# Depthwise convolution of a Conformer stage: four of eight chunks without TensorE blocks, and the whole stage in one written order

## The chip, the cores and the metric

The kernel runs on one core of one Trainium2 chip. The metric is the device time of one execution in microseconds (us), the median of several runs. The engines named below are TensorE (PE in the profile, its weight loads PEld), VectorE (DVE), ScalarE (ACT), GpSimd (POOL) and SyncE (SP, which here only issues DMAs). Each engine works through its own queue of instructions in order; semaphores tie the queues together.

## The reference, cut to what matters

A trunk of two layers over 512 positions of 1024 channels, batch 1, all in fp32. The change touches the first part of layer 1, the Conformer module:

```python
def conformer_conv(x, norm, w1, b1, dw_w, dw_b, ln_g, ln_b, w2, b2):
    h = rms_norm(x, norm) @ w1 + b1      # 1024 -> 2048
    h = jax.nn.glu(h, axis=-1)           # value half * sigmoid(gate half)
    h = causal_dwconv(h, dw_w, dw_b)     # width 31, each channel by itself
    h = jax.nn.silu(layer_norm(h, ln_g, ln_b))
    return h @ w2 + b2
```

Each layer then has a cross-attention into 256 memory tokens, whose keys and values (`m @ wk`, `m @ wv`) depend on the memory alone and can be computed ahead, and a gated MLP.

## The kernel before

**Layout.** Channels lie on partitions, positions along the free axis: 1024 channels are 8 chunks of [128, 512]. Matrix products keep fp32 accuracy by splitting both operands into a high part (fp32r, rounded) and a low part (the residual) and adding three matmuls, `mm3` (lines 183 to 185). A weight piece of 128 output channels, [128, 1024], passes through `load_w`: a DMA on SP into `raw` (3 buffers, line 149), a copy on ScalarE for the high part (line 163), a subtraction on VectorE or GpSimd for the low part (line 164), into `whi` and `wlo` (4 buffers each). A piece that is "parked" is split in two halves of 512 into the pool `act` (32 tiles) instead.

**Scheduling.** Outside of `manual_schedule` blocks a scheduler orders each engine's instructions by priority. Inside such a block the listed engines issue exactly in the order in which the code writes the instructions.

**The stage.** `conformer` follows the first layer's MLP. In order:

- Four weight pieces of `pw1` are split (gate and value half of chunks 0 and 1), and four of the eight key pieces for the next cross-attention, parked during the MLP, are multiplied (`mem.keys`). Beside them the RMS norm is formed (`Scaled`): scale (VectorE, line 265), high part (ScalarE, line 173), low part (VectorE, line 178), one chunk after the other.
- `project` multiplies one piece with the eight normed chunks: 24 matmuls of 512 columns. The gate half goes through a sigmoid with its bias on ScalarE (`gate`, line 1349). `gated` multiplies the value half with it on VectorE into a tile `h` with four spare columns in front (line 1362); GpSimd clears those four columns (line 1361).
- The 31 taps of chunk c are shared out. `PE_GROUPS[c]` groups of four taps go to TensorE: `gated` makes four stacked copies of `h` by DMA (`actf<-h`, line 1369, on SP), each with one 32-channel quarter four times, shifted by 0 to 3 positions (they read three of the cleared columns); `spread` builds the matching small diagonal weights on GpSimd (line 1381); `conv_pe` runs 4 matmuls a group into a PSUM bank (line 1391; these are fp32 and show as two records each). The next `N_POOL` taps are products on ScalarE (lines 1410 and 1413) which GpSimd adds into a tile z (line 1414). The rest are taps on VectorE, each a multiply-add onto the PSUM bank (line 1416). `merge` adds bank, bias and z (line 1425). The banks of the convolution come from the pool `aux`, which has two.
- With `PE_GROUPS = [3, 2, 3, 2, 3, 3, 3, 8]` and 5 taps aside for chunks 0 to 6, VectorE has 14 or 18 taps of each of the first seven chunks, 106 in all, and none of the last, whose 31 taps all lie on TensorE. VectorE and GpSimd cannot begin a chunk's PSUM part before its TensorE block.
- The last part is in a manual schedule: keys 6 and 7, the last block, then the LayerNorm over channels. Its sums (`quarters`, line 293; `mu`, then `mean`, line 1497) need all eight merged chunks; between its steps TensorE works through `mem.sums` (line 442), the products of the next cross-attention's value weights `wv`, pieces 0 to 7 (`mem.piece`). After the first sums VectorE subtracts the mean (line 1499) and ScalarE squares (line 1501).

Of the kernel before, what the change touches and what calls it, by code (L numbers as in the profile page):

```python
# [15 lines left out]
P = 128  # L16
# [19 lines left out]
PE_GROUPS = [3, 2, 3, 2, 3, 3, 3, 8]  # L36
N_POOL = [5] * 7 + [0]
LAG = 5

KE = 4  # L40
WINDOWS = (2, 4, 8, 16)
# [5 lines left out]
    ("c_dw_w", (TAPS - 4 * min(PE_GROUPS)) * C), ("c_dw_b", C), ("c_ln_g", C), ("c_ln_b", C), ("c_b_pw2", C),  # L47
# [12 lines left out]
def trunk(ctx: ExitStack, tc: tile.TileContext, I: dict, out: list):  # L60
# [173 lines left out]
    class Scaled:  # L234


        def __init__(self, gain):
            self.gain, self.x, self.ss = gain, [None] * C, None

        def feed(self, c):  # L240
            sq = tmp_f()
            A.activation(sq, X[c], AF.Square)
# [26 lines left out]
        def high(self, c):  # L269
            self.x[c] = self.x[c], high(self.x[c])  # L270
# [18 lines left out]
    def quarters(ps, xs):  # L289

        def quarter(j):
            n = len(xs) - 4 + j
            return PE.matmul(ps[32 * j : 32 * j + 32], onesf[:, :32], xs[n], start=n < 4, stop=n >= 4)


        with tc.issue_after(quarter(3).ins):
            for j in range(3):
                quarter(j)
# [500 lines left out]
    def ffn(layer, norm, nxt, seven):  # L799
# [267 lines left out]
        if nxt:  # L1067
            mem = Memory(1)
            mem.operand(0)
            mem.operand(1)  # L1070
            mem.outputs()
            parked = []
            for n in range(KE):
# [268 lines left out]
    def conformer(norm, nxt, mem, parked):  # L1342
# [4 lines left out]
        def gate(c, psb):  # L1347
            b = tmp_f()
            A.activation(b, psb, AF.Sigmoid, bias=col("c_b_pw1", C + c))
            return b  # L1350

        def pieces(c):
            return load_w(I["pw1"][C + c], V if c == 2 else G), load_w(I["pw1"][c], G)

        def glu(c, w):
            b = gate(c, project(w[0], c, norm.x))
            gated(c, b, project(w[1], c, norm.x))

        def gated(c, b, psa):
            h = tmp.tile([P, T + 4], F32, tag="h", name=nm("h"), bufs=4)  # L1360
            G.memset(h[:, :4], 0.0)
            V.scalar_tensor_tensor(h[:, 4:], psa, col("c_b_pw1", c), b, op0=ALU.add, op1=ALU.mult)
            stacked = [act_f() for _ in range(4)]
            for j in range(4):

                v = h[32 * j : 32 * j + 32, 1 : 1 + T].unsqueeze(1).broadcast_to([32, 4, T])
                dims = [list(d) for d in v.ap]
                dims[1][0] = 1
                nc.sync.dma_start(stacked[j], bass.AP(v.tensor, v.offset, dims))
            hs[c] = h[:, 4:], stacked  # L1370

# [31 lines left out]
        def conv(c):  # L1403
            h, ps = hs[c][0], accs[c]
            z = act_f()
            first = 4 * PE_GROUPS[c]
            for s in range(first, first + N_POOL[c]):
                if s == first:
                    G.memset(z[:, :s], 0.0)
                    A.activation(z[:, s:], h[:, : T - s], AF.Copy, scale=tap(s, c))  # L1410
                else:
                    f = tmp_f()
                    A.activation(f[:, s:], h[:, : T - s], AF.Copy, scale=tap(s, c))
                    G.tensor_tensor(z[:, s:], z[:, s:], f[:, s:], op=ALU.add)
            for i, s in enumerate(range(first + N_POOL[c], TAPS)):
                V.scalar_tensor_tensor(ps[:, s:], h[:, : T - s], tap(s, c), ps[:, s:], op0=ALU.mult, op1=ALU.add)
                if i == LAG and pend:
                    merge(*pend.pop())
            if pend:
                merge(*pend.pop())  # L1420
            pend.append((c, z, ps))

        def merge(c, z, ps):
            if N_POOL[c]:
                V.scalar_tensor_tensor(z, ps, col("c_dw_b", c), z, op0=ALU.add, op1=ALU.add)
            else:
                A.activation(z, ps, AF.Identity, bias=col("c_dw_b", c))
            outs.append(z)
            if c % 4 == 3:
                quarters(mu, outs)  # L1430

        pend, taps = [], [None] * C
        accs = [None] * C
        w = [load_w(I["pw1"][n]) for n in (C, 0, C + 1, 1)]
# [5 lines left out]
        spread(0)  # L1440
        spread(1)
        with tc.high_priority(URGENT):
            for c in range(C):
                norm.split(c)
        ps = project_all(w[:3], norm.x)
        gated(0, gate(0, ps[0]), ps[1])
        gated(1, gate(1, ps[2]), project(w[3], 1, norm.x))
        mu = stat_ps()
        w = pieces(2)
        for c in range(C - 1):  # L1450
            b = None
            if c == 0:
                b = gate(2, project(w[0], 2, norm.x))
            if c == 1:
                gated(2, gate2, project(w[1], 2, norm.x))
                w = pieces(3)
            elif c > 1:
                glu(c + 1, w)
                if c < C - 2:
                    w = pieces(c + 2)  # L1460
            gate2 = b
            if c in (0, C - 2):
                mem.keys(KE + c // 6)
            conv_pe(c)
            if c < C - 2:
                spread(c + 2)
            conv(c)
        xs = [None] * C
        with tc.manual_schedule(engines=ORDERED):
            w = [mem.key_piece(n) for n in (KE + 2, KE + 3)]  # L1470
            mem.eng = G
            ready = [mem.piece(i, park=True) for i in range(3)]
            for n in range(2):
                mem.keys(KE + 2 + n, w[n])
            ready.append(mem.piece(3, park=True))
            last = conv_pe(C - 1)
            ps = [[mm_ps(), mm_ps()] for _ in range(2)]
            z = act_f()
            A.activation(z, accs[C - 1], AF.Identity, bias=col("c_dw_b", C - 1))
            merge(*pend.pop())  # L1480
            outs.append(z)
            mem.eng = None
            ready += [mem.piece(i) for i in (4, 5)]
# [7 lines left out]
            quarters(mu, outs)  # L1491
# [6 lines left out]
            for c in range(C):  # L1498
# [3 lines left out]
                if c == 3:  # L1502
                    go(3)
                    quarters(var, sqs)
# [3 lines left out]
            quarters(var, sqs)  # L1508
# [214 lines left out]
def _layout(inputs):  # L1723
# [3 lines left out]
    a["c_dw_w"] = a["c_dw_w"][:, : TAPS - 4 * min(PE_GROUPS)]  # L1727
# [51 lines left out]
```

## Time and profile before

| | us |
|---|---|
| median of 3 runs | 1447.76 |
| the three runs | 1447.96, 1447.76, 1445.3 |
| the profiled execution | 1445.47 |
| its span, first to last instruction | 1443.0 |
| TensorE busy in the span | 1433.5 |
| first projection of the stage begins | 745.0 |
| last convolution block ends | 870.6 |
| last sum of the mean begins | 873.6 |

The page of the profile is read by sections: section 1 gives the busy time of each engine, a table by stretches the same for parts of the span with the granted TensorE clock (1.00 is full speed), the chain of waits the work that ended last at each moment, and the lists in order of time each engine's instructions: start, length, line, output and inputs, count, and in brackets the idle time before and what ended it. TensorE's instructions are pipelined, so a new one begins before the last ends; the pitch from start to start is what counts. The same holds, more weakly, for VectorE and ScalarE.

### The profile page before, as it was taken

To read this page: it belongs to the slowest core of one execution; us is meant where nothing else is said; L and a number is where in the kernel's file an instruction comes from. 1 tells how busy PE (TensorE), PEld (TensorE's weight loads), DVE (VectorE), ACT (ScalarE), POOL (GpSimd) and SP (SyncE) were. 2 spreads that over 40 slices of the span, in tenths; PEclk is the share of its full clock that TensorE was granted. 3 is DMA by queue.
4 is the path that set the end of the run, shared out by engine and by line. 5 is a ranking of instruction groups with operands and counts; after the bars stand their busy time and mean duration, and the time that the engine had idled before them with its cause. 6 is when DMAs were issued, how large, how long until landed. Compare 5 with 4: busy or idle time off the path is not lost.

```text
span 1443.0 us, 22827 instructions
## 1 busy us (share of the span) xinstructions
PE 1433.5 (99%) x8608; PEld 1260.1 (87%) x8608; DVE 1162.5 (81%) x1916; ACT 787.3 (55%) x1305; POOL 274.8 (19%) x307
## 2 busy tenths in 40 slices
PE   9999999999999999999999999999999999999997
PEld 8888888988899999999887676899888999999997
DVE  6987775768788888888875897878788888888885
ACT  7668754657544444444545447666664444444433
POOL 0012300100022212212006841010001222221201
PEclk9999999999999999999999999999999999999999
DMA  8522232532567777876526654335245777777741
GB/s 303 190 88 89 89 130 73 125 96 88 161 151 166 185 157 166 181 168 146 158 88 177 165 155 151 112 81 138 90 124 128 173 183 159 168 182 163 160 126 59
DMA packets 80398, 205.33 MB, mean 142 GB/s; under 512 B 8992, under 2 KB 10272, under 8 KB 80288
## 3 DMA queue, kind: packets, MB, share of 16 engines
q1 hardware_dynamic: 53504, 155.36, 34.6%
q0 software_dynamic: 26496, 48.25, 20.4%
q8 instruction: 67, 1.10, 0.3%
q14 instruction: 43, 0.35, 0.1%
q10 hardware_dynamic: 288, 0.27, 0.1%
HBM read 145.13 MB, written 2.10 MB: 102 GB/s over the span
## 4 chain that ended last, share of the span: by engine, by line
PE 95%; DVE 2%; ACT 1%; DMA 1%; issue 0%; POOL 0%; SPq 0%; DVEq 0%; POOLq 0%; ACTq 0%
PE mm L183 23%; PE mm L184 23%; PE mm L185 23%; PE aux L183 7%; PE aux L184 7%; PE aux L185 7%; PE mm L442 3%; PE aux L1391 2%; PE aux L515 0%; DMA raw<-in_wv 0%; DVE wlo L164 0%; POOL tmp L1234 0%; DMA raw<-in_wdown 0%; ACT whi L163 0%; PE stat L316 0%
## 5 line engine op out<-in xcount | busy, mean ns | idle before, releaser
L183 PE MATMUL mm<-act,whi 128*128 128x512 f32 (+2 forms) x1093 | 385.3, 354 | 0.3 <-ACT act L849 0.3
L184 PE MATMUL mm<-act,whi 128*128 128x512 f32 (+2 forms) x1093 | 385.0, 352 | 0.1
L185 PE MATMUL mm<-act,wlo 128*128 128x512 f32 (+2 forms) x1093 | 384.7, 352 | 0.0
L183 PEld LDWEIGHTS mm<-act,whi 128*128 128x128 f32 x1093 | 206.3, 189 | 35.1 <-issue 3.3
L184 PEld LDWEIGHTS mm<-act,whi 128*128 128x128 f32 x1093 | 206.6, 189 | 29.4 <-DVE act L164 1.0
L185 PEld LDWEIGHTS mm<-act,wlo 128*128 128x128 f32 x1093 | 206.6, 189 | 27.1
L779 ACT ACTIVATE bigr<-raw 128x512 fp32r<-128x512 f32 x160 | 100.5, 629 | 158.5 <-DMA raw<-wa 67.8
L185 PE MATMUL mm<-bigr,bigr 128*128 128x256 f32 x640 | 181.1, 283 | 0.0
L184 PE MATMUL mm<-bigr,bigr 128*128 128x256 f32 x640 | 181.1, 283 | 0.0
L183 PE MATMUL mm<-bigr,bigr 128*128 128x256 f32 x640 | 180.9, 283 | 0.0
L168 DVE TENSOR_TENSOR tmp<-mm,tmp 128x256 f32<-128x256 f32 x322 | 130.9, 419 | 34.1 <-PE mm L185 27.8
L183 PE MATMUL aux<-act,whi 128*128 128x512 f32 x399 | 156.3, 392 | 0.0
L184 PE MATMUL aux<-act,whi 128*128 128x512 f32 x399 | 156.2, 392 | 0.0
L185 PE MATMUL aux<-act,wlo 128*128 128x512 f32 x399 | 155.2, 389 | 0.0
L163 ACT ACTIVATE whi<-raw 128x1024 fp32r<-128x1024 f32 (+1 forms) x95 | 96.2, 1019 | 96.7 <-PE mm L184 64.7
L786 DVE TENSOR_TENSOR bigr<-raw,bigr 128x512 fp32r<-128x512 f32 x160 | 109.9, 688 | 33.3 <-ACT bigr L779 31.2
L164 DVE TENSOR_TENSOR wlo<-raw,whi 128x1024 fp32r<-128x1024 f32 (+1 forms) x84 | 103.0, 1230 | 31.5 <-ACT whi L163 31.4
L184 PEld LDWEIGHTS mm<-bigr,bigr 128*128 128x128 f32 x640 | 122.7, 192 | 1.6
L183 PEld LDWEIGHTS mm<-bigr,bigr 128*128 128x128 f32 x640 | 122.7, 192 | 1.6
L185 PEld LDWEIGHTS mm<-bigr,bigr 128*128 128x128 f32 x640 | 122.7, 192 | 0.0
L789 POOL DMA_DIRECT2D raw<-raw x46 | 39.8, 866 | 359.3 <-DVE wlo L786 316.0
L793 POOL DMA_DIRECT2D raw<-wa x46 | 39.7, 864 | 302.4 <-DVE bigr L786 252.5
(338 smaller groups left out, 2958.4 us busy)
## 6 DMA issues: line engine op xcount, KB each, us to landing
raw<-wa POOLq DMA_DIRECT2D x138, 256.0 KB, 4.5
big<-in_wdown SPq DMA_DIRECT2D x42, 512.0 KB, 6.7
wa<-in_wpair SPq DMA_DIRECT2D x80, 256.0 KB, 3.4
raw<-in_wpair SPq DMA_DIRECT2D x40, 512.0 KB, 5.7
raw<-in_pw SPq DMA_DIRECT2D x24, 512.0 KB, 3.5
raw<-raw POOLq DMA_DIRECT2D x46, 256.0 KB, 7.5
raw<-in_win SPq DMA_DIRECT2D x20, 512.0 KB, 3.3
raw<-in_wk SPq DMA_DIRECT2D x16, 512.0 KB, 4.2
```

The lines of the kernel that those rows point to most:

```text
L163: A.activation(hi, src, AF.Copy)
L164: fetched[1] = (eng or V).tensor_tensor(lo, src, hi.bitcast(F32), op=ALU.subtract)
L168: V.tensor_tensor(out, a, b, op=ALU.add)
L183: PE.matmul(ps, wh, xh, start=first, stop=False)
L184: PE.matmul(ps, wh, xl, start=False, stop=False)
L185: PE.matmul(ps, wl, xh, start=False, stop=last)
L442: PE.matmul(p, m[j], x, start=k == 0 and j == 0 and x is hi, stop=k == C - 1 and x is lo)
L779: A.activation(self.w[name][0], self.block(name), AF.Copy)
L786: V.tensor_tensor(lo, self.block(name), hi.bitcast(F32), op=ALU.subtract)
L789: G.dma_start(self.r, self.z, accum_op=ALU.add)
L793: G.dma_start(self.r, self.a22, accum_op=ALU.add)
L1391: return PE.matmul(accs[c][32 * j : 32 * j + 32, s:], taps[c][:, 4 * g + j], hs[c][1][j][:, : T - s], start=s == 0, stop=g == PE_GROUPS[c] ...
```

## The change

It rewrites the stage up to the LayerNorm.

- **The sharing of taps.** `PE_GROUPS` becomes `[0, 0, 4, 0, 4, 0, 3, 6]`: chunks 0, 1, 3 and 5 have no block, no diagonal weights and no stacked copies. VectorE begins them itself, by a product of tap 0 written to the bank, and does 26 taps; ScalarE and GpSimd do five taps aside for every chunk, the last too. All 31 taps' weights are loaded in columns.
- **The stacked copies** are issued on ScalarE's queue instead of SP's.
- **The norm** has its instructions on VectorE and ScalarE in a written order: scale of chunk c + 1 between scale and low part of chunk c. Two empty activations load the square root's and the sigmoid's tables ahead.
- **Weights.** The splits of all pieces from the fifth on, the last four key pieces among them, lie on GpSimd; of the value pieces, 0 and 1 are split there whole, 2 and 3 parked there, 4 and 5 parked on VectorE.
- **One order.** Projections, sigmoids, GLU products, taps, taps aside, merges, blocks, keys and weight splits of the whole stage stand in one manual schedule on TensorE, ScalarE, VectorE and GpSimd, written as a script. Its letters: G and V are the gate and value projection of a chunk (G with its sigmoid), S the GLU product with the clearing and the four stacked copies, T a number of VectorE taps, P a number of taps aside, M the merge, F the split of the next weight piece on GpSimd, C the TensorE block, W its diagonal weights, K a key product, Q a half of the mean's sums. The first digit is the chunk, the rest a count.

```diff
-PE_GROUPS = [3, 2, 3, 2, 3, 3, 3, 8]
-N_POOL = [5] * 7 + [0]
-LAG = 5
+PE_GROUPS = [0, 0, 4, 0, 4, 0, 3, 6]
+N_POOL = 5
...
-        def gated(c, b, psa):
+        def gated(c):
             h = tmp.tile([P, T + 4], F32, tag="h", name=nm("h"), bufs=4)
-            G.memset(h[:, :4], 0.0)
-            V.scalar_tensor_tensor(h[:, 4:], psa, col("c_b_pw1", c), b, op0=ALU.add, op1=ALU.mult)
-            stacked = [act_f() for _ in range(4)]
-            for j in range(4):
-
+            if PE_GROUPS[c]:
+                G.memset(h[:, :4], 0.0)
+            V.scalar_tensor_tensor(h[:, 4:], psa[c], col("c_b_pw1", c), b[c], op0=ALU.add, op1=ALU.mult)
+            stacked = []
+            for j in range(4 if PE_GROUPS[c] else 0):
+                stacked.append(act_f())
                 v = h[32 * j : 32 * j + 32, 1 : 1 + T].unsqueeze(1).broadcast_to([32, 4, T])
                 dims = [list(d) for d in v.ap]
                 dims[1][0] = 1
-                nc.sync.dma_start(stacked[j], bass.AP(v.tensor, v.offset, dims))
+                A.dma_start(stacked[j], bass.AP(v.tensor, v.offset, dims))
             hs[c] = h[:, 4:], stacked
+            aside[c] = set_aside(c)
...
+        def shifts(c):
+            ss = list(range(4 * PE_GROUPS[c], TAPS))
+            at = 0 if PE_GROUPS[c] else 1
+            return ss[at : at + N_POOL], ss[:at] + ss[at + N_POOL :]
...
+        def conv(c):
+
+            h, (_, own) = hs[c][0], shifts(c)
+            ps = accs[c] = accs[c] or aux_ps()
+            for s in own:
+                if s:
+                    V.scalar_tensor_tensor(ps[:, s:], h[:, : T - s], tap(s, c), ps[:, s:], op0=ALU.mult, op1=ALU.add)
+                else:
+                    V.tensor_scalar(ps, h, tap(s, c), None, op0=ALU.mult)
+                yield
...
-        with tc.high_priority(URGENT):
+        with tc.high_priority(URGENT), tc.manual_schedule(engines={mybir.EngineType.Activation, mybir.EngineType.DVE}):
+            norm.scaled(0)
             for c in range(C):
-                norm.split(c)
...
+                norm.high(c)
+                if c + 1 < C:
+                    norm.scaled(c + 1)
+                norm.low(c)
+        warm("gates", AF.Sigmoid, norm.copied[3])
...
+            run("S0 G1 F0 P02 F0 P03 T015 V1 F0 S1 T011 P12 F0 G2 P13 F0 T15 M0 V2 S2 W4 F0 P22 G3 F0 P23")
+            run("T114 V3 S3 T17 F0 C2 P32 G4 F0 P33 T25 M1 T25 T34 V4 S4 F0 P42 T31 M2 G5 F0 P43 W6 T313 V5 S5 F0 P52")
+            run("T38 C4 T45 M3 T45 G6 F0 P53 T53 V6 S6 F0 P62 T52 M4 Q0 G7 F0 P63 W7 T516 V7 S7 F0 P72 T55 C6")
+            run("T63 K4 P73 T62 M5 K5")
+            ready = [mem.piece(i) for i in range(2)]
+            run("T64 K6 C7 T65 M6 T72 M7 K7")
+            ready += [mem.piece(i, park=True) for i in (2, 3)]
             ps = [[mm_ps(), mm_ps()] for _ in range(2)]
-            z = act_f()
-            A.activation(z, accs[C - 1], AF.Identity, bias=col("c_dw_b", C - 1))
-            merge(*pend.pop())
-            outs.append(z)
             mem.eng = None
-            ready += [mem.piece(i) for i in (4, 5)]
+            ready += [mem.piece(i, park=True) for i in (4, 5)]
             steps = mem.sums(0, ps[0], ready)
```

More of the change, by code (lines that the diff above doesn't have):

```diff
@@ L1072, in ffn @@
             parked = []
-            for n in range(KE):
+            for n in range(PARKED):
                 if n + 1 < C // 2:
@@ L1449, in conformer @@
[L1449 to L1467, printed above, removed]
+                norm.high(c)
@@ L1468, in conformer @@
+                if c + 1 < C:
+                    norm.scaled(c + 1)
+                norm.low(c)
+        warm("gates", AF.Sigmoid, norm.copied[3])
         xs = [None] * C
+        mem.eng = G
         with tc.manual_schedule(engines=ORDERED):
[L1470 to L1475, printed above, removed]
@@ L1476, in conformer, with run @@
-            last = conv_pe(C - 1)
+            ps0 = project_all([ws["G0"], ws["V0"]], norm.x)
+            mu = stat_ps()
+            def run(script):
+                for step in script.split():
+                    k, c, n = step[0], int(step[1]), int(step[2:] or 0)
+                    if k == "G":
+                        sigmoid(c, project(ws[step], c, norm.x))
+                    elif k == "V":
+                        psa[c] = project(ws[step], c, norm.x)
+                    elif k == "S":
+                        gated(c)
+                    elif k == "T":
+                        convs[c] = convs[c] or conv(c)
+                        for _ in range(n):
+                            next(convs[c])
+                    elif k == "P":
+                        for _ in range(n):
+                            next(aside[c])
+                    elif k == "M":
+                        assert next(convs[c], True) and next(aside[c], True)
+                        merge(c)
+                    elif k == "F":
+                        weights(G)
+                    elif k == "C":
+                        conv_pe(c)
+                    elif k == "W":
+                        spread(c)
+                    elif k == "K":
+                        mem.keys(c, ws.get(step, parked[c] if c < PARKED else None))
+                    elif k == "Q":
+                        quarters(mu, outs, c)
```

90 lines of the change are left out of this document (41 added, 49 removed).

## The prediction

> **What bounds the kernel now.** I read the page first, then the table by stretches over the convolution stage, then the chain of waits through it, then each engine's instructions in time.
>
> ```profile
> span 1443.0 us, 22827 instructions
> PE 1433.5 (99%) x8608; PEld 1260.1 (87%) x8608; DVE 1162.5 (81%) x1916; ACT 787.3 (55%) x1305; POOL 274.8 (19%) x307
> ```
>
> ```profile
> core 0: us, PE busy (x) PEld busy (x) DVE busy (x) ACT busy (x) POOL busy (x), PEclk, DMA share, GB/s
> 800.00:820.00 20.00, 20.00 (x96) 15.11 (x96) 18.59 (x30) 7.90 (x12) 17.02 (x15) 1.00 0.76 208
> ```
>
> TensorE has hardly a gap, so a microsecond of TensorE work taken out is a microsecond won, if nothing else makes TensorE wait. In this stage two engines stand right behind it: VectorE at 18.6 of 20 and GpSimd at 17.0 of 20. ScalarE looks free, but only as long as nothing in its queue has to wait. The median of the runs, 1447.76, lies 2.3 us above the profiled execution's 1445.47, and the lowest run 0.2 below it. My sum is made against 1445.47; the 2.3 goes into the range.
>
> **TensorE's part.** The chain gives the durations.
>
> ```profile
> 785.49 0.43 PE mm L183
> ...
> 796.64 2.69 PE aux L1391 x24
> ...
> 857.84 0.32 PE mm L183
> ...
> 863.78 6.82 PE aux L1391 x64
> 870.60 2.99 PE mm L442 x12
> 873.59 1.00 PE stat L293 x8
> 874.58 1.59 PE mm L442 x6
> 876.17 0.86 PE aux L1497 x2
> 877.03 4.12 PE mm L442 x18
> ```
>
> A convolution block of three groups takes 2.69, of eight 6.82: (6.82 - 2.69) / 5 = 0.83 a group and 0.2 besides. The first matmul after a block takes 0.43 where its neighbours take 0.23: 0.2 more. Between 785.49 and 796.64 lie two projections: (11.15 - 0.2) / 2 = 5.45 each. Two key products lie between 857.84 and 863.78: 2.9 each. Before, groups 3, 2, 3, 2, 3, 3, 3, 8 make 27 x 0.83 + 8 x 0.2 = 24.0. After, 4, 4, 3, 6 make 17 x 0.83 + 4 x 0.2 = 14.9. That is 9.1 less, and four switches fewer save 0.8: **9.9 us off TensorE**, the whole gain.
>
> **VectorE's part.** Taps rise from 106 to 140, and the last chunk's sum comes over from ScalarE.
>
> ```profile
> 784.35 8.48 DVE L1416 SCALAR_TENSOR_TENSOR aux<-h,par,aux 128x488 f32<-128x488 f32 x13
> 792.75 0.74 DVE L1425 SCALAR_TENSOR_TENSOR actf<-aux,par,actf 128x512 f32<-128x512 f32 x1
> 793.41 2.27 DVE L1416 SCALAR_TENSOR_TENSOR aux<-h,par,aux 128x493 f32<-128x493 f32 x3
> ...
> 877.54 4.86 DVE L1499 TENSOR_TENSOR actf<-actf,aux 128x512 f32<-128x512 f32 x8
> ```
>
> ```profile
> L1416 DVE SCALAR_TENSOR_TENSOR aux<-h,par,aux 128x491 f32<-128x491 f32 (+16 forms) x106 | 72.4, 727 | 3.6 <-PE aux L1391 2.3
> ```
>
> A tap lasts 0.727, but each begins before the last has ended: thirteen start 8.4 before the merge, 0.65 a tap, and 0.66 for a merge or a GLU product (792.75 to 793.41). The new taps are four chunks of 26, two of 10, one of 14, one of 2. 140 x 0.65 + 16 x 0.66 + 4 key residuals under 0.5 = 103 us. The new chunks need no block, so VectorE begins when chunk 0's two products are there. The projections start here:
>
> ```profile
> 745.02 0.40 PE L183 MATMUL mm<-act,whi 128*128 128x512 f32 x1
> ```
>
> Two products instead of three: 745.0 + 10.9 = 755.9. 756.3 + 103 = 859.3, beside TensorE's 755.9 + 104.5 = 860.4 for the same stretch (14 projections, blocks, four keys, one sum). Balanced with no room: VectorE hides its 34 taps only if it never stands still. The norm's pitch falls from three instructions in turn (scale, copy, residual) to VectorE's two, some 1.3, and its table loads move ahead. Both gain nothing by themselves: the first four keys hold TensorE until 745.0, and six matmuls a chunk (5.45 / 4 = 1.36) then consume no faster than that. Without the pipelining the copy's 0.6 and its hand-overs would stand in each chunk's pitch, and two products at a time would wait up to 8 x 0.7 = 5.6.
>
> **GpSimd and ScalarE: where the change adds waits.** These rows price them.
>
> ```profile
> 798.79 2.41 POOL L164 TENSOR_TENSOR wlo<-raw,whi 128x1024 fp32r<-128x1024 f32 x1
> 801.12 0.12 POOL L1409 MEMSET actf<- 128x12 f32 x1
> 801.19 5.30 POOL L1414 TENSOR_TENSOR actf<-actf,tmp 128x499 f32<-128x499 f32 x4
> 806.44 2.42 POOL L164 TENSOR_TENSOR wlo<-raw,whi 128x1024 fp32r<-128x1024 f32 x1
> ...
> 863.76 7.51 POOL L164 TENSOR_TENSOR act<-raw,act 128x512 fp32r<-128x512 f32 x6
> ```
>
> ```profile
> 792.55 2.50 ACT L1413 ACTIVATE tmp<-h,par 128x499 f32<-128x499 f32 x4
> 796.45 1.06 ACT L163 ACTIVATE whi<-raw 128x1024 fp32r<-128x1024 f32 x1 [1.40 <-PE mm L184]
> 797.41 0.70 ACT L1410 ACTIVATE actf<-h,par 128x500 f32<-128x500 f32 x1
> ...
> 863.82 0.38 ACT L163 ACTIVATE bigr<-mm 128x256 fp32r<-128x256 f32 x1 [2.49 <-PE mm L185]
> ...
> 872.52 1.06 ACT L163 ACTIVATE whi<-raw 128x1024 fp32r<-128x1024 f32 x1 [0.21 <-DMA raw<-in_wv]
> 874.74 0.60 ACT L1493 ACTIVATE tmp<-stat 128x512 f32<-128x512 f32 x1 [1.15 <-PE stat L293]
> ```
>
> ```profile
> 786.52 4.31 SPq L1369 DMA_DIRECT2D actf<-h  x4
> ```
>
> ```profile
> L1369 SPq DMA_DIRECT2D actf<-h x32: 554/890/1922, 766.4 to 855.8; - x32
> ```
>
> ```profile
> actf<-h SPq DMA_DIRECT2D x32, 256.0 KB, 4.8
> ```
>
> A weight residual on GpSimd takes 2.33 (798.79 to 801.12), an add 1.31 (801.19 to 806.44 for four). A weight copy on ScalarE takes 0.96, a tap copy 0.6. GpSimd's queue now holds 20 pieces (15 before) and 32 adds (28): 18 x 2.33 + 4 x 1.25 + 32 x 1.31 + spreads of 4 = 93 us in a stage of 100.
>
> In that queue stands the clearing of four columns of h, written inside the GLU step. The stacked copies read those columns. They were issued by SP, whose wait held up weight loads only; now ScalarE issues them, and waits in its written order. Behind it there: the next weight copy (GpSimd's next residual waits for it), the tap copies, the next sigmoid (VectorE's next GLU product waits), and in the end the keys' copies.
>
> Chunk 2: G1 ends at 761.4, its sigmoid and the copy of G2 take ScalarE to 763.2, and GpSimd starts then. Written ahead of the clearing are five residuals and eight adds: 5 x 2.33 + 8 x 1.31 + 0.2 = 22.3, so it comes at 785.7. VectorE has h ready at 779.4. Four issues take 4.31: if the first two take the shortest, some 0.6, the others take 1.55, and the last starts 2.7 in, at 788.6, and lands 4.8 later, at 793.4. TensorE reaches the block at 788.6: **4.9 us of stall**. An issue of 0.55 or 1.92 throughout would give 3.8 or 7.9; I take the burst's 4.31, which is this very transfer.
>
> From there GpSimd and ScalarE hold each other up in turn: each burst (4.3) and the next weight copy (1.0) leave GpSimd idle. Next residual 791.2; four residuals and eight adds (19.8) and two or three clears and gaps: clearing for chunk 4 at 811.5. Burst and copy to 816.9; as much again with chunk 6's spread: 838.0. Burst and copy to 843.4; two residuals, four adds, a spread of 2: chunk 7's clearing at 855.5. Its burst ends at 859.8; K7's weights and two tap copies follow, and only at 862.3 is key 4's high part out of ScalarE. VectorE, which has stood before key 4's residual since 853.2, then does it, two taps and chunk 5's merge: 864.7. Chunk 7's block needs the bank that this merge frees. TensorE is there at 793.5 + 63.7 (two blocks of 3.73, eight projections, the sum, a block of 2.9, three keys) = 857.2: **7.5 us of stall**.
>
> The mean: key 7 ends, then follow in written order ScalarE's copy of it (0.5), a piece of wv in two copies, its residuals on GpSimd (0.6 + 2 x 1.25), the load of piece 5 into that buffer, piece 5's two copies, and the copy of the sums. From the buffer's release to the first copy took 3.75 in the run before: of the six residuals from 863.76, at 1.25 each, the fourth ends piece 2 at 868.8, and the copy of piece 5, three buffers on, starts at 872.52. In all 0.5 + 0.6 + 2.5 + 3.75 + 1.1 + 0.6 and some 0.2 of hand-overs = 9.3, against 2.99 + 1.00 + 1.59 = 5.6 on TensorE: **3.7 us**. Piece 6's residual then delays the eight subtractions (0.6 each) behind the 4.12 of products: **1.1**.
>
> Sum: -9.9 + 4.9 + 7.5 + 3.7 + 1.1 = +7.3; 1445.5 + 7.3 = **1452.8**, rounded to 1453. Free are the 16 stacked copies fewer on SP (it only waits less) and the 64 more columns of parameters, loaded at the start and not read before 756.
>
> One rule speaks for a smaller price. The Trainium skill, "DMA: Bandwidth & Descriptors", section "Issuing engines are not separate DMA queues", says that issuing on another engine saves only the sequencer's time to initiate, usually small beside the transfer. The burst's 4.31 beside 4.8 is not small; by the rule the bursts would hold ScalarE little, and the sum would be that of the short issues below, 1446.7.
>
> **The rivals.** *The clearing does not bind* (the copies go out as soon as h is there). Then the first two stalls vanish, the last two stay: -9.9 + 4.8 = -5.1, **1440.4**, faster. For it: VectorE and TensorE are balanced at 859 to 860; against it: the rows' 22.3 us of GpSimd work. It decides once the clearing comes within 5 us after h. If the wv pieces come early too, it is the full -9.9, 1435.6.
>
> *Short issues*: four at about 0.6 on ScalarE's own queue. Bursts shrink by 1.9, chunk 7's clearing comes at 851.2, key 4's copy at 856.2, the merge ends at 858.5, and TensorE is there at 856.2: stalls 4.0 + 2.3 + 3.7 + 1.1 = 11.1 against 9.9, **1446.7**, no change. Against it: SP's burst, the same transfers with nothing else in between.
>
> *VectorE becomes the bound* without the coupling: if the taps did not overlap, at 0.727, it would end 140 x 0.077 = 11 us later. The blocks wait for banks that its merges free, and the sums for its last merge, so all of it but the 2 or 3 us that TensorE's products behind the last block cover comes through, some 8.5; the last two stalls stay: -9.9 + 8.5 + 4.8 = +3.4, **1448.9**. It loses from a pitch of 0.70 on. The 8.48 for thirteen speaks against it.
>
> *TensorE's clock falls in the gaps.* Each window above grants 1.00, but none has a gap; after gaps of 4.9 and 7.5, the blocks behind them (3.7 and 5.4) could run at half speed, 0 to +9.1, middle **1457**. The Trainium skill, "TensorE: Matmul & The Clock Gate", section "HAM oscillation — how this bites in real kernels", says that idle gaps over about 3.4 us halve the clock; no run here shows it.
>
> **How the numbers follow.** Coupling as summed 0.42 (its own range 1449 to 1456); coupling and slow clock 0.13; VectorE 0.05; short issues 0.13; clearing not binding 0.20; full gain 0.07. 0.2% is about 2.9 us, what a measurement of this kernel can tell from no change. Faster: 0.27; same: 0.13; slower: 0.60. The range from 1440 to 1457.5 takes in the first rival and the middle of the last; the full gain, half of the slow clock and issues of 1.92 (+21) stay out.
>
> **What would show it.** Right: in the changed profile TensorE idles before chunk 2's and chunk 7's blocks, released by the stacked copies and by VectorE; ScalarE idles before its issues, released by a GpSimd memset some 6 us after VectorE wrote h; GpSimd idles before residuals, waiting for ScalarE's copies; VectorE idles some 9 us before key 4's residual; the mean stands 3 to 4 us late. Wrong: blocks that start at once, memsets that run early, a burst of four below 2.5 us, or taps at another pitch than 0.65.

## The result, and the profile after

| | us | to the kernel before |
|---|---|---|
| before, median of 6 runs | 1446.39 | |
| after, median of 6 runs | 1458.84 (1458.23 to 1459.39) | 1.0085 [1.0072, 1.0098] |
| after, the profiled execution | 1458.82 | 13.35 above the profiled execution before |

The change makes the kernel slower by 12.45 us. The direction was predicted; the time lies 6 above the predicted 1453 and 1.3 above the end of the range.

The page of the changed kernel: span and busy time of each engine.

```profile
span 1457.0 us, 22652 instructions
PE 1431.0 (98%) x8528; PEld 1259.7 (86%) x8528; DVE 1186.3 (81%) x1948; ACT 789.0 (54%) x1311; POOL 287.3 (20%) x307
```

TensorE has less to do than before (1433.5) and the span is 14 longer: it waits, where before it hardly did. What TensorE waited for between 740 and 900, with the total, the number and the longest wait:

```profile
PE aux L1389 <- DVE actf L1432: 7.0, 1, 7.0
PE aux L1389 <- DMA actf<-h: 4.9, 2, 4.6
PE aux L1525 <- ACT tmp L1521: 3.3, 1, 3.3
PE aux L295 <- ACT tmp L1529: 0.3, 1, 0.3
```

The first three are the three large stalls of the prediction: 4.9 before chunk 2's block was forecast and 4.6 came, 7.5 before chunk 7's and 7.0 came, 3.7 before the mean and 3.3 came. The last is what came of its fourth term, 1.1 behind the mean. The instructions in time show the mechanism (start, length, engine, line, operation; idle time before and its releaser in brackets):

```profile
745.97 0.40 PE L183 MATMUL mm<-act,whi 128*128 128x512 f32 x1
...
786.51 0.10 POOL L1358 MEMSET h<- 128x4 f32 x1
786.64 4.33 ACTq L1366 DMA_DIRECT2D actf<-h  x4
794.30 5.30 PE L1389 MATMUL aux<-actf,big 128*32 128x512 f32 x32 [4.63 <-DMA actf<-h]
...
857.55 0.11 POOL L1358 MEMSET h<- 128x4 f32 x1
857.69 4.33 ACTq L1366 DMA_DIRECT2D actf<-h  x4
864.21 0.36 ACT L163 ACTIVATE bigr<-mm 128x256 fp32r<-128x256 f32 x1
864.61 0.42 DVE L164 TENSOR_TENSOR bigr<-mm,bigr 128x256 fp32r<-128x256 f32 x1 [3.06 <-ACT bigr L163]
866.35 0.75 DVE L1432 SCALAR_TENSOR_TENSOR actf<-aux,par,actf 128x512 f32<-128x512 f32 x1
867.20 8.05 PE L1389 MATMUL aux<-actf,big 128*32 128x512 f32 x48 [7.02 <-DVE actf L1432]
...
886.96 2.08 PE L1525 MATMUL aux<-tmp,fourth 128*128 128x512 f32 x2 [3.32 <-ACT tmp L1521]
```

GpSimd clears the four columns at 786.5 (forecast 785.7), ScalarE issues its four copies at once and is held for 4.33 (forecast 4.31), the block starts at 794.3 (793.4). In the end the same chain frees chunk 7's bank: clearing, burst, key 4's copy, its residual, chunk 5's merge. It runs 2.0 to 2.5 later than forecast. Two of the signs that the prediction named came out much smaller: the clearing for chunk 2 stands 2.9 behind the end of VectorE's product, not some 6, and VectorE stands 3.06 before key 4's residual, not some 9. VectorE is later than the prediction had it: that product ends at 783.6, not at 779.4.

Two rows were not in the sum. The first is the length of the blocks. Four groups should take 3.5, six 5.2; they took 5.30 and 8.05. The table by stretches has the reason in its column PEclk (after the stretch, its length and five engines' busy times comes the granted clock, then DMA share and GB/s):

```profile
core 0: us, PE busy (x) PEld busy (x) DVE busy (x) ACT busy (x) POOL busy (x), PEclk, DMA share, GB/s
786.00:788.00 2.00, 2.00 (x11) 1.65 (x10) 1.93 (x3) 0.00 (x0) 1.62 (x3) 1.00 0.32 33
...
796.00:798.00 2.00, 2.00 (x16) 0.70 (x12) 1.89 (x4) 2.00 (x4) 2.00 (x1) 0.56 0.51 203
...
870.00:872.00 2.00, 2.00 (x12) 0.46 (x8) 1.96 (x4) 0.00 (x0) 2.00 (x2) 0.50 0.00 0
...
888.00:890.00 2.00, 2.00 (x5) 1.29 (x4) 0.43 (x1) 1.06 (x1) 0.00 (x0) 0.52 1.03 416
```

After each of the three gaps the clock stands at 0.5 to 0.6 for some microseconds, and the work behind the gap runs on it.

The second is the pitch of the taps. In the view of one line's instructions, between 784 and 793, the kernel before has these thirteen taps (shortest, median and longest duration in ns, first and last start, shapes):

```profile
L1416 DVE SCALAR_TENSOR_TENSOR aux<-h,par,aux x13: 716/729/735, 784.4 to 792.1; 128x488 f32<-128x488 f32 x1, 128x487 f32<-128x487 f32 x1, 128x499 f32<-128x499 f32 x1, 128x486 f32<-128x486 f32 x1
```

and the changed kernel these:

```profile
L1426 DVE SCALAR_TENSOR_TENSOR aux<-h,par,aux x13: 732/739/744, 783.5 to 792.8; 128x502 f32<-128x502 f32 x1, 128x501 f32<-128x501 f32 x1, 128x500 f32<-128x500 f32 x1, 128x499 f32<-128x499 f32 x1
```

A tap lasts the same, but twelve intervals take 7.7 before (0.65 each with the first, 0.64 without) and 9.3 after (0.775 each). The shapes tell the two apart. A tap at shift s works on 512 - s positions. Before, 488 and 487 are one chunk's; from there on the taps of two chunks take turns (487, 499, 486, ...). After, 502, 501, 500, 499 are one chunk's, each adding onto the bank that the last one writes. In the program such a tap carries a wait for VectorE's own count of the tap before it. The first taps of the row of before, one by one (the last line holds two taps), have both pitches already:

```profile
784.35 0.72 DVE L1416 SCALAR_TENSOR_TENSOR aux<-h,par,aux 128x488 f32<-128x488 f32 x1
785.11 0.73 DVE L1416 SCALAR_TENSOR_TENSOR aux<-h,par,aux 128x487 f32<-128x487 f32 x1
785.75 1.37 DVE L1416 SCALAR_TENSOR_TENSOR aux<-h,par,aux 128x499 f32<-128x499 f32 x2
```

From 488 to 487, in one chunk, it is 0.76; from 487 to 499, to the other chunk, 0.64. At 0.775 the 140 taps would take some 108 us, not 91 (an estimate: a few of them follow an instruction of another chunk). In the chain of waits from 780 to 900 VectorE's taps have the largest share:

```profile
by line: DVE aux L1426 37.3%; issue 14.5%; ACTq L1366 6.9%; PE aux L1389 6.7%; POOL act L164 4.3%; ACT tmp L1529 3.8%; ACT whi L163 3.5%; POOL actf L1417 2.9%; DMA raw<-in_wv 2.6%; DVE h L1359 2.4%; DVE actf L1432 2.3%; ACT tmp L1416 2.0%; 
```

That leaves two suspects for the loss, the late clearing and the dependent taps, and a third, the clock, for the 6 us between sum and result.

### The profile page after: what moved, and what is told of

Its sections match the earlier page's. It is cut to its first block, busy times and chain, and to the rows that moved or that the text cites. A ratio compares the mean times of both kernels' runs of the same rounds, so it can differ in the third digit from the quotient of the medians.

```text
span 1457.0 us, 22652 instructions
## 1 busy us (share of the span) xinstructions
PE 1431.0 (98%) x8528; PEld 1259.7 (86%) x8528; DVE 1186.3 (81%) x1948; ACT 789.0 (54%) x1311; POOL 287.3 (20%) x307
## 4 chain that ended last, share of the span: by engine, by line
PE 85%; DVE 7%; ACT 2%; issue 2%; DMA 2%; POOL 1%; ACTq 1%; SPq 0%; DVEq 0%; POOLq 0%
PE mm L183 20%; PE mm L185 20%; PE mm L184 20%; PE aux L183 7%; PE aux L184 7%; PE aux L185 7%; DVE aux L1426 4%; PE mm L444 1%; DMA raw<-in_wv 1%; ACT whi L163 1%; ACTq L1366 1%; DVE wlo L164 1%; PE aux L1389 1%; PE aux L517 0%; DMA raw<-wa 0%
## 5 line engine op out<-in xcount | busy, mean ns | idle before, releaser
L164 DVE TENSOR_TENSOR wlo<-raw,whi 128x1024 fp32r<-128x1024 f32 (+1 forms) x77 | 93.2, 1214 | 25.6 <-ACT whi L163 25.4
L1426 DVE SCALAR_TENSOR_TENSOR aux<-h,par,aux 128x482 f32<-128x482 f32 (+24 forms) x136 | 99.5, 734 | 4.3
```

Source lines behind the costliest of these rows:

```text
L164: fetched[1] = (eng or V).tensor_tensor(lo, src, hi.bitcast(F32), op=ALU.subtract)
```

## The experiments

All are edits of the changed kernel. Ratios are to the kernel before, with 95% intervals; differences are of medians.

### The two suspects, one at a time and together

*Cleared early:* the tile is taken, and cleared, when the gate projection is written.

```diff
+            hp[c] = tmp.tile([P, T + 4], F32, tag="h", name=nm("h"), bufs=4)
+            if PE_GROUPS[c]:
+                G.memset(hp[c][:, :4], 0.0)
...
         def gated(c):
-            h = tmp.tile([P, T + 4], F32, tag="h", name=nm("h"), bufs=4)
-            if PE_GROUPS[c]:
-                G.memset(h[:, :4], 0.0)
+            h = hp[c]
```

> The buffer h of each chunk is taken, and its four leading columns are cleared by GpSimd, when the gate projection of the chunk is written, so that the copies no longer wait for the clearing; all else is as in the changed kernel (profiled 1458.8). Theory A, two locks: the late clearing and the dependent taps of VectorE (0.775 each in place of the 0.65 of the prediction) each hold the stage alone. Then VectorE keeps nearly all of the loss: adding up rows along the written order gives 2.5 less, so 1454 to 1458; the copies start at about 779 to 780, the 4.6 before the block of chunk 2 shrink to 1 to 2, and a gap of 4 to 6 stays before the block of chunk 7, ended by the merge of chunk 5. Theory B, the coupling of the prediction was the whole loss and the taps have room: both gaps go and the time falls by 12 to 18, to 1441 to 1447.

Measured: 1455.67, 1.0062 [1.0049, 1.0074], 3.2 less than the changed kernel. TensorE's waits:

```profile
PE aux L1390 <- DVE actf L1433: 5.0, 1, 5.0
PE aux L1390 <- DMA actf<-h: 4.8, 2, 3.7
```

The copies of chunk 2 now start right behind the GLU product, but that product comes at 782.1, behind sixteen taps that depend on one another, not at 779.4; the gap shrinks only to 3.7, more than the 1 to 2 expected. Chunk 7's block still waits 5.0 for chunk 5's merge. Theory B (coupling alone) falls.

*Alternating taps:* a new letter X takes taps of two open chunks in turn (X0105: five of chunk 0 and five of chunk 1); some 90 of the 140 then follow a tap of the other chunk. The last T65 becomes T63.

```diff
-            run("S0 G1 F0 P02 F0 P03 T015 V1 F0 S1 T011 P12 F0 G2 P13 F0 T15 M0 V2 S2 W4 F0 P22 G3 F0 P23")
-            run("T114 V3 S3 T17 F0 C2 P32 G4 F0 P33 T25 M1 T25 T34 V4 S4 F0 P42 T31 M2 G5 F0 P43 W6 T313 V5 S5 F0 P52")
-            run("T38 C4 T45 M3 T45 G6 F0 P53 T53 V6 S6 F0 P62 T52 M4 Q0 G7 F0 P63 W7 T516 V7 S7 F0 P72 T55 C6")
-            run("T63 K4 P73 T62 M5 K5")
+            run("S0 G1 F0 P02 F0 P03 T015 V1 F0 S1 X0103 P12 F0 G2 P13 F0 X0105 V2 S2 X0103 M0 W4 F0 P22 G3 F0 P23")
+            run("T16 V3 S3 T19 F0 C2 P32 G4 F0 P33 M1 X3207 V4 S4 F0 P42 X3203 M2 G5 F0 P43 W6 T39 V5 S5 F0 P52")
+            run("T33 C4 X4304 M3 X5404 G6 F0 P53 V6 S6 F0 P62 X5402 M4 Q0 G7 F0 P63 W7 T58 V7 S7 F0 P72 T55 C6")
+            run("X6504 K4 P73 X6503 M5 K5")
```

> Only the order of the taps on VectorE is changed: wherever two chunks are open in two banks, their taps alternate, so that 90 of 140 taps follow a tap of another chunk. The clearing stays where the change has it. Theory A, two locks: the alternating taps follow each other at 0.64 to 0.66 and the ones of a single chunk at 0.77 to 0.78; VectorE gets about 11.5 of room and the time does not move (1456 to 1461), since the clearing, the burst of copies and the key copy behind it still start when GpSimd lets them; VectorE idles instead. Theory C, VectorE alone binds and the late clearing is harmless: 7 less, about 1452. Theory D, the pitch of 0.775 is not from the dependence on the tap before but belongs to this kernel (reads of the bank beside TensorE's writes, say): the alternating taps keep 0.77.

Measured: 1460.31, 1.0095 [1.0081, 1.0109], 1.5 more than the changed kernel. The alternating taps of chunks 0 and 1, and two of VectorE's idle times:

```profile
L1426 DVE SCALAR_TENSOR_TENSOR aux<-h,par,aux x14: 724/732/744, 771.5 to 779.8; 128x491 f32<-128x491 f32 x1, 128x506 f32<-128x506 f32 x1, 128x490 f32<-128x490 f32 x1, 128x505 f32<-128x505 f32 x1
```

```profile
794.11 0.75 DVE L1359 SCALAR_TENSOR_TENSOR h<-mm,par,tmp 128x512 f32<-128x512 f32 x1 [3.90 <-ACT tmp L1353]
...
863.28 0.42 DVE L164 TENSOR_TENSOR bigr<-mm,bigr 128x256 fp32r<-128x256 f32 x1 [5.33 <-ACT bigr L163]
```

Thirteen intervals in 8.3 are 0.64 a tap. In the same run, fourteen taps of chunk 0 alone, ahead of these:

```profile
L1426 DVE SCALAR_TENSOR_TENSOR aux<-h,par,aux x14: 735/744/750, 758.8 to 768.9; 128x506 f32<-128x506 f32 x1, 128x505 f32<-128x505 f32 x1, 128x504 f32<-128x504 f32 x1, 128x503 f32<-128x503 f32 x1
```

They take 10.1 for thirteen intervals, 0.777 each: theory D falls, the pitch is the dependence. The time gained is stood out, 3.9 before chunk 3's GLU product and 5.3 before key 4's residual, both behind ScalarE. Theory C (taps alone) falls. The 1.5 more fit the new order, which has six taps between key 4's residual and chunk 5's merge where the change has two: the merge starts at 867.6, not 866.35.

*Both:*

> Both edits together: cleared early and taps alternating. Theory A, two locks: neither edit alone moves the time by more than 3, both together take away 9 by the sum of the rows and 2 to 4 of lost TensorE clock with the gaps, so 1445 to 1449; a gap of about 4 stays before the block of chunk 7 (merge of chunk 5) and the 3.3 before the mean. Theory B (coupling alone): no more than the early clearing by itself. If the gains of the two edits just add up, there are no two locks.

Measured: 1449.59, 1.0022 [1.0012, 1.0031], 9.3 less than the changed kernel, 0.6 over the end of the expectation. Alone the edits give -3.2 and +1.5; together -9.3. That is the mark of two locks in a row: each holds the stage when the other is opened.

### The clock

Matmuls that nobody reads fill TensorE's three gaps.

```diff
+        def fill(n):
+            ps = mm_ps() if n else None
+            for _ in range(n):
+                PE.matmul(ps, onesf, X[0], start=True, stop=True)
...
         def conv_pe(c):
 
+            fill({2: 5, 7: 8}.get(c, 0))
             accs[c] = aux_ps()
...
+            fill(3)
             PE.matmul(mean, fourth, f, start=True, stop=True)
```

> The changed kernel with matmuls whose result nobody reads put into TensorE's three gaps: 5 (128x512 float32, about 0.86 each at the mean's row) ahead of the block of chunk 2, 8 ahead of that of chunk 7, 3 ahead of the mean. They wait for nothing and end before or about when the awaited data come. Theory E, the clock that falls after a gap is a cost of its own: the granted clock stays at 1.0 through the blocks, the block of chunk 2 takes 3.5 in place of 5.3, that of chunk 7 5.2 in place of 8.05, and the time falls by 3 to 6 (to 1453 to 1456), less where VectorE sets the end anyway. Rival: the low clock hides behind VectorE and costs nothing, time 1457 to 1460 even though the clock stays up.

Measured: 1456.49, 1.0069 [1.0056, 1.0082], 2.4 less than the changed kernel, a little under the smallest gain expected. The blocks, and a stretch inside the second:

```profile
794.38 3.60 PE L1395 MATMUL aux<-actf,big 128*32 128x512 f32 x32 [0.28 <-DMA actf<-h]
...
867.43 5.26 PE L1395 MATMUL aux<-actf,big 128*32 128x512 f32 x48 [0.33 <-POOL actf L1423]
```

```profile
868.00:870.00 2.00, 2.00 (x25) 0.66 (x20) 1.89 (x4) 1.01 (x2) 1.84 (x3) 1.00 0.22 90
```

With the array kept busy the clock stays at 1.00 and the blocks take 3.60 and 5.26, as the rows of before gave them (3.5 and 5.2). Chunk 2's 1.7 were hidden (chunk 7's block starts at 867.4, in the changed kernel at 867.2, because VectorE and ScalarE set it: chunk 5's merge begins at 866.6 here and at 866.35 there); chunk 7's 2.8 and the mean's 1.0 were on the path, but not all of them arrive: TensorE now waits 0.8 before the variance, where it waited 0.3.

Then the clock and the taps mended as far as an order can, the coupling left alone (nine fillers before chunk 7):

> The changed kernel with the late clearing and the burst on ScalarE left as they are, but with the two things taken away that the prediction's sum did not hold: matmuls nobody reads in the gaps (5, 9 and 3) keep TensorE's clock up, and the taps alternate. Theory: what is left is the coupling as the prediction summed it, 1452.8, and the 0.8 by which TensorE starts the stage late: 1452 to 1455. Rival: the coupling itself costs more than was summed, and the time stays at that of the filled gaps alone, 1456 to 1458.

Measured: 1455.47, 1.0063 [1.0050, 1.0075], half a microsecond over the expectation. The chain to chunk 7's block, in time:

```profile
854.87 0.10 POOL L1358 MEMSET h<- 128x4 f32 x1
...
861.42 0.36 ACT L163 ACTIVATE bigr<-mm 128x256 fp32r<-128x256 f32 x1
...
861.81 0.42 DVE L164 TENSOR_TENSOR bigr<-mm,bigr 128x256 fp32r<-128x256 f32 x1 [4.84 <-ACT bigr L163]
862.15 3.88 DVE L1432 SCALAR_TENSOR_TENSOR aux<-h,par,aux 128x491 f32<-128x491 f32 x6
866.13 0.75 DVE L1438 SCALAR_TENSOR_TENSOR actf<-aux,par,actf 128x512 f32<-128x512 f32 x1
```

With the pitch that the prediction assumed, the clearing comes at 854.9 (forecast 855.5) and key 4's copy at 861.4 (862.3). The merge is late again only through the six taps of this order: two in their place, at 0.65, would bring the time 2.6 lower, to 1452.9 beside the sum's 1452.8. This last step is an estimate from these rows, with all of the 2.6 on the path; it was not run.

### The mean's wait, and the copies back on SyncE

Pieces 5 and 6 go behind the first four subtractions.

```diff
-            ready += [mem.piece(i, park=True) for i in (4, 5)]
+            ready += [mem.piece(4, park=True)]
...
-            ready.append(mem.piece(6))
...
                     quarters(var, sqs, 0)
+                    ready += [mem.piece(5, park=True), mem.piece(6)]
```

> The changed kernel, with pieces 5 and 6 of the value projection moved behind the first four subtractions of the normalization, so that ScalarE's copy of the sums and VectorE's subtractions no longer queue behind copies that wait for their pieces to land. Theory: the 3.3 before the matmul of the mean go, with the 1 to 1.5 of lost clock behind it, and the 1.1 of piece 6's residual ahead of the subtractions: 1452.5 to 1455. Rival: the pieces are then late for the second half of the value sums, or the wait goes to another place (the sums of the mean wait for the merge of chunk 7), and no more than 1 is gained (1457.5 to 1459).

Measured: 1457.13, 1.0080 [1.0068, 1.0093], 1.7 less, between the two expectations. The wait before the mean is gone, and all of it comes back at the variance, with the low clock behind it:

```profile
867.67 6.55 PE L1389 MATMUL aux<-actf,big 128*32 128x512 f32 x48 [7.07 <-DVE actf L1432]
...
894.10 1.87 PE L295 MATMUL aux<-tmp,onesf 128*32 128x512 f32 x8 [3.91 <-ACT tmp L1528]
```

The copies of pieces 5 and 6 now stand ahead of the second four squares. From the first value product (877.1 here, 878.1 in the changed kernel) to the matmuls behind the variance's sums (898.2 and 899.3) the profiled execution gains 0.1. What it gains ahead of that is chunk 7's block: 6.55 after the same gap of 7, where the changed kernel's execution took 8.05. So the move by itself is worth next to nothing here, which is the rival, and the length of the low clock differs between executions.

One part of the change undone, the stacked copies issued by SyncE:

```diff
-                A.dma_start(stacked[j], bass.AP(v.tensor, v.offset, dims))
+                nc.sync.dma_start(stacked[j], bass.AP(v.tensor, v.offset, dims))
```

> One part of the change undone: the four copies of a chunk are issued by SyncE, as in the kernel before, not by ScalarE; the clearing is still late. If the 4.2 to 4.3 in which ScalarE issues a chunk's copies are what holds key 4's copy out and with it the merge of chunk 5, key 4's copy comes 3 to 4 earlier and the gap of 7.0 before the block of chunk 7 shrinks to 3 to 5: 1455 to 1457. Rival: SyncE holds the loads of weights in order, each waiting for a free buffer, and the copies queue behind them; then the gaps before the blocks of chunks 2, 4 or 6 grow and the time rises by 2 or more (over 1461).

Measured: 1462.77, 1.0116 [1.0103, 1.0130], 3.9 more: the rival. In time:

```profile
790.81 4.61 SPq L1366 DMA_DIRECT2D actf<-h  x4
...
821.64 4.43 SPq L1366 DMA_DIRECT2D actf<-h  x4
```

The clearing for chunk 2 comes at 786.9, 0.4 later than in the changed kernel, but the copies start 3.9 behind it, after loads that wait for free buffers, and chunk 2's block waits 9.1. In this order the move to ScalarE was worth its burst.

### Mended, and each lock put back

Cleared early, alternating taps (S2 one pair earlier, two of chunk 5's taps ahead of V7), and a main bank for chunk 7's block.

```diff
-            accs[c] = aux_ps()
+            accs[c] = mm_ps() if c == C - 1 else aux_ps()
```

> Cleared early and alternating taps as in the run of both, with the second chunk's gate and a few taps shifted by one place, and the block of chunk 7 accumulating in one of the five main banks, so that it needs no merge of chunk 5. By the sum of the rows the gap of 3 to 4 before the block of chunk 7 goes (3.3 less), with some 2 of lost clock: 1443.5 to 1447, about the kernel before. If that gap was hidden (VectorE's last merges set the mean anyway), 1448 to 1450.

Measured: 1442.88, 0.9979 [0.9970, 0.9988]: faster than the kernel before by 3.1. TensorE's waits:

```profile
PE aux L1528 <- ACT tmp L1524: 1.8, 1, 1.8
PE stat L295 <- DVE actf L1433: 1.7, 1, 1.7
PE aux L295 <- ACT tmp L1532: 1.2, 1, 1.2
PE mm L1390 <- DMA actf<-h: 0.4, 1, 0.4
```

None is over 2, and each stretch of 20 us between 780 and 920 grants 1.00. From this version each suspect can be priced by itself. The taps back in the change's order:

> The version with everything mended (cleared early, alternating taps, block of chunk 7 in a main bank; 1442.9) with the taps put back into the order of the change, one chunk after the other. It prices the dependence of the taps by itself, with no coupling: 10 more by the sum of the rows, and up to 3 of clock, since gaps open before the blocks: 1452 to 1456. If only the coupling counts, 1443 to 1446.

Measured: 1454.31, 1.0053 [1.0039, 1.0067]: **11.4 for the dependent taps alone**, a little over the sum of rows, with chunk 7's block at 7.99 on a low clock again. TensorE's waits before the blocks (the longest in `aux` is chunk 2's, `mm` is chunk 7's):

```profile
PE aux L1390 <- DMA actf<-h: 4.6, 2, 3.9
PE mm L1390 <- DMA actf<-h: 4.2, 1, 4.2
```

The clearing back in the GLU step:

> The version with everything mended (1442.9) with the clearing put back into the GLU step. It prices the coupling by itself, with taps that overlap: 10.5 more by the sum of the rows, and up to 3 of clock: 1453 to 1457. If only the taps count, 1443 to 1446.

Measured: 1455.75, 1.0063 [1.0050, 1.0075]: **12.9 for the late clearing alone**. The same waits:

```profile
PE aux L1389 <- DMA actf<-h: 4.4, 1, 4.4
PE mm L1389 <- DMA actf<-h: 4.0, 1, 4.0
```

The changed kernel, with both and without the main bank, lies 16.0 above this version: either lock by itself costs most of that.

What was left were the copies of the value pieces. Moved as in the run above:

> The run before it, with pieces 5 and 6 of the value projection behind the first four subtractions as well. If the wait before the mean is on the path, 3 to 5 less than the run before it: 1439 to 1443, below the kernel before (1446.4). If the gain only moves the wait, the same as the run before it within 1.

Measured: 1444.17, 0.9985 [0.9976, 0.9994], no gain on 1442.88 (1.3 more, with runs from 1441.64 to 1446.62): the mean's wait is gone and 2.9 stand before the variance. Moved further:

```diff
-            ready += [mem.piece(i, park=True) for i in (4, 5)]
+            ready += [mem.piece(4, park=True)]
...
-            ready.append(mem.piece(6))
...
-            ready.append(mem.piece(7))
+            ready.append(mem.piece(5, park=True))
...
             A.activation(f, var, AF.Copy)
+            ready += [mem.piece(6), mem.piece(7)]
```

> Cleared early, alternating taps, the block of chunk 7 in a main bank, and of the value pieces only piece 4 before the copy of the mean's sums; piece 5 goes behind the eight subtractions and squares, 6 and 7 behind the copy of the variance's sums. If the waits of 1.8 before the mean and of 2.9 before the variance come only from copies that wait for their pieces, both go: 1440 to 1442. If the pieces are then late for the second half of the value sums, 1443 to 1446.

Measured: **1438.46, 0.9943 [0.9930, 0.9955]**, better than expected and 7.9 below the kernel before. One stretch of it:

```profile
780.00:800.00 20.00, 20.00 (x105) 14.30 (x105) 19.40 (x30) 9.17 (x13) 19.69 (x15) 1.00 0.50 157
```

TensorE is full here, VectorE and GpSimd just behind it. Of the 9.9 that the change takes off TensorE, 7.9 arrive.

## Why the prediction was right and where it was wrong

**The gain of 9.9 off TensorE** was right as work: the version mended furthest gets 7.9 of it, and small waits are left in it (the largest 1.7, before the mean's sums).

**The coupling** (clearing behind GpSimd's queue, burst on ScalarE, key 4's copy, chunk 5's merge) was right in its place, and its stalls came near in size: 4.6 and 7.0 against 4.9 and 7.5. That the late clearing costs this much is shown by the clearing put back alone (+12.9). There chunk 7's block lies in a main bank and waits for its own copies; the last two links, key 4's copy and chunk 5's merge, are shown only by the changed kernel's rows. The size is in part luck: VectorE came late too, and with the clearing early the same two gaps were still 3.7 and 5.0. (One sum is 0.2 off: 763.2 + 22.3 is 785.5. It changes nothing.) The rival *short issues* fell with a burst of 4.33. The rule quoted for it is in the Trainium skill, "DMA: Bandwidth & Descriptors", section "Issuing engines are not separate DMA queues": the time to initiate is usually small beside the transfer. It does not fit these copies: initiating one took 1.1 of the 4.8 from its issue to its landing, and the four together held ScalarE for 4.33.

**"A tap lasts 0.727, but each begins before the last has ended: thirteen start 8.4 before the merge, 0.65 a tap"** failed. The row was read as one chunk's taps; all but its first pair are two chunks' in turn, and the change puts them in sequence. The price is 0.775, by the estimate above 17 us more on an engine that was forecast "balanced with no room". In the changed kernel this is mostly hidden behind the coupling: the chain to chunk 7's block runs 2 later. But it decides the rivals. *The clearing does not bind*, 1440.4 at a chance of 0.20, could not happen: cleared early, the kernel takes 1455.67. *VectorE becomes the bound*, at a chance of 0.05 because "the 8.48 for thirteen speaks against it", is what the run cleared early and the taps put back alone (+11.4) show; forecast at +3.4, it measured +9.3 (cleared early) on the kernel before, low clock included.

**"TensorE's clock falls in the gaps"** was held for a rival at 0.13 and left out of the sum. Leaving it out is the step that failed: it is what happened, and it carries most of the miss: the profiled execution was forecast 7.3 above that of before and came 13.35 above. Along TensorE's instructions: 0.9 late into the stage (745.97 against 745.02; among four runs above whose code is the same up to there, chunk 0's GLU product starts between 756.4 and 757.5, so much of this moves from one execution to the next), some 1.6 more up to chunk 7's block, 2.8 in that block and 1.0 at the mean (clock), less 0.4 of smaller stalls. The 1.6 belong to taps and clock together: chunk 7's clearing, at 857.55, comes 1.25 earlier with the taps alternating, no earlier with the gaps filled, and 2.7 earlier with both. The 1.0 is what is left after the fourth term, 1.1, came as a wait of 0.3: the slow products behind the mean cover the rest of it. Filled gaps give 2.4 of the clock's 3.8 back. The Trainium skill, "TensorE: Matmul & The Clock Gate", section "HAM oscillation — how this bites in real kernels", has the clock halve after idle gaps of more than some 3.4 us; the gaps of 4.6 and 7.0 agree, that of 3.32 lost the clock too, and the rest is below.

**The mean's wait** was right in size (3.3 against 3.7), and its cause (copies that wait for pieces to land, in a queue in order) is shown by the runs that moved them: the wait goes wherever such a copy stands ahead of something that TensorE needs, and only in the last version does it go without coming back.

**The norm's pipelining** was put at nothing and was not tried by itself.

## What to carry to other kernels

Before a pitch is taken from a row of many instructions, look at what alternates in it: a chain of adds onto one bank took 0.775 an add here, two chains in turn 0.64. Where several queues in order are balanced, price each lock with the others opened, for an edit that opens one of two gains little and its cause looks refuted. And a forecast stall on TensorE can cost more than its length: behind most of the gaps of 2 us and more in these runs, the work ran on a fallen clock.

## What the runs showed of the hardware that was not expected

- VectorE starts a tap some 0.09 before the last one of 0.73 ends when it needs nothing of it, and some 0.04 after the end when it does: 0.64 and 0.775 a tap in the same kernel. The Trainium skill, "VectorE: DVE Perf Modes", section "The DRAIN you can't avoid", says that the next instruction waits for the pipeline to empty, and that a semaphore between the two costs nothing extra. In these runs a tap that waits for the one just before it comes a fifth later than one that waits for none so near.
- The clock fell after shorter gaps than expected, though not after every one. In the run with both edits a gap of 1.97 before chunk 2's block was enough:

```profile
792.02 5.30 PE L1390 MATMUL aux<-actf,big 128*32 128x512 f32 x32 [1.97 <-DMA actf<-h]
```

```profile
790.00:792.00 2.00, 0.05 (x1) 0.01 (x1) 1.96 (x4) 2.00 (x4) 2.00 (x4) 1.00 0.60 204
792.00:794.00 2.00, 1.98 (x16) 0.76 (x20) 1.93 (x3) 1.83 (x4) 2.00 (x2) 0.80 0.51 190
794.00:796.00 2.00, 2.00 (x13) 0.61 (x9) 1.89 (x4) 0.58 (x1) 1.92 (x2) 0.50 0.50 137
```

  The clock is still full through the gap and falls some 1.2 into the block (0.80 over the two microseconds from 792, full before and 0.50 behind). With the copies on SyncE a gap of 2.33 before chunk 7's block brought it to 6.95, but one of 2.54 before chunk 4's block left its 3.60 whole. Before the mean, a gap of 3.32 in the changed kernel made its two matmuls take 2.08; one of 3.31 in the run cleared early left them at 1.13. So the length of the gap alone does not tell the cases apart, and what does was not tried.
